# A two-block transformer on one core: the modulation's matrix-vector product moves from VectorE and GpSimd to ScalarE and GpSimd, and to other stages

## Chip, cores and metric

One Trainium2 chip, one of its cores. The metric is the device time of one execution in microseconds (us). Five engines run side by side: TensorE (PE, with its weight loads as PEld), VectorE (DVE), ScalarE (ACT), GpSimd (POOL) and SyncE (SP), whose queue issues the DMAs of this kernel. Each engine works through its own instructions in a fixed order; semaphores hold it until what it needs is there. An "issue" of a DMA stands in SP's order just like an instruction.

## What is computed

1024 tokens of width 1024 in fp32 pass through a first block (differential attention over 4 heads, neighbourhood attention over 8 heads, an output projection, a gate) and then through two layers of a second block. Each of those layers is modulated by a vector that depends on the condition `c` alone:

```python
c_act = jax.nn.silu(c)                                   # (1, 1024)
for l in range(DEPTH_2):                                 # 2 layers
    mod = c_act @ w_mod[l] + b_mod[l]                    # (1, 6144); w_mod[l] is 1024 x 6144
    sh1, sc1, gt1, sh2, sc2, gt2 = jnp.split(mod, 6, axis=-1)
    h = rms_norm_2(x, g_norm_mix[l]) * (1.0 + sc1[:, None]) + sh1[:, None]
    ...                                                  # dilated attention, latent attention (MLA)
    x = x + gt1[:, None] * mix
    h = rms_norm_2(x, g_norm_mlp[l]) * (1.0 + sc2[:, None]) + sh2[:, None]
    y = jnp.square(jax.nn.relu(h @ w_mlp_in[l])) @ w_mlp_out[l]
    x = x + gt2[:, None] * y
```

The change concerns `c_act @ w_mod[l]`, 2 x 24 MB of weights that are read once.

## The kernel before

The stages follow each other: set-up; differential attention (`diff_groups`); neighbourhood attention (`na_groups`); output projection and gate of the first block (`block1_end`); then for each layer dilated attention, latent attention (`mla`), an output projection and the MLP with an up and a down part. All large products run as three passes of split fp32 ("hi" and "lo" tiles): ACT casts a tile to its hi part (`split`, L127, tiles named `ph` in the attention stages), DVE subtracts to get the lo part (L128, `pl`), and PE uses both. In the attention stages a group goes through scores on PE, a minimum on DVE (`add_min`, L493, `mn`), an exponential on ACT, transposes on PE, `split`, and the product with the values on PE.

A modulation *piece* (`mod_piece`) is 256 rows by 256 columns of `w_mod`, 256 KB: one DMA into a tile `modraw` (two chunks of 128 rows), a multiplication of each chunk by its column of `csil` (silu of `c`), and sums into an accumulator `macc` of 128 x 256. Four pieces (kh = 0 to 3) make a column of 256 outputs, 24 columns a layer, 2 layers: 192 pieces. After the fourth piece two transposes of `macc` on PE (L155) and a reduction on DVE (L161) add up the 128 rows, and L974 adds the result to `mod`.

Pieces wait in a list (`background`), and `run_background(n)` writes down the next n of them at a given point of the program. Before the change: 2 after each of the 16 groups of the differential attention and 1 after each of the 16 groups of the neighbourhood attention; 3 in each of the 16 steps (`side`) of output projection and gate; 8 for each of the up part's loops in layer 0's MLP. So the first 48 pieces run in block 1's attention, 48 in its projection and gate, and layer 1's 96 in layer 0's MLP. In the differential attention they are multiplied (L960) and added (L962, L963) on POOL, everywhere else on DVE, which multiplies and adds in one instruction (L967 for the first chunk, L969).

`side` also makes the position tables of the dilated attention: 32 tiles `tab` on DVE (L1156), which have two buffers and leave by the DMA `acd<-tab`. The output projection adds its result to the stream on DVE (L872, tile `xT`).

The order on each engine is not written by hand: a scheduler places every instruction by the program's order as priority and by when it finds its inputs and buffers free. It may so place a piece earlier than the point where the program writes it.

## Time and profile before

| | us |
|---|---|
| median of 3 runs | 3877.02 (3874.85 to 3882.91) |
| the profiled execution | 3880.11 |
| its span | 3878.2 |
| PE busy in it | 3613.2 (93%) |
| DVE | 2821.6 (73%) |
| ACT | 1842.2 (48%) |
| POOL | 1565.9 (40%) |
| layer 0's MLP, layer 1's MLP (from the last instruction of the projection, L874, to the last of L1831) | 1714.8 to 2437.9, 3176.4 to 3871.3 |

Matmuls are pipelined, so a busy PE says little by itself; a stage's length, and what PE waits for in it, say more. "A <- B" in a row means that A waited for B. The two layers of the second block are the same program on other weights, which makes them comparable stage by stage.

### The profile page before, as it was taken

To read this page: it belongs to the slowest core of one execution; us is meant where nothing else is said; L and a number is where in the kernel's file an instruction comes from. 1 tells how busy PE (TensorE), PEld (TensorE's weight loads), DVE (VectorE), ACT (ScalarE), POOL (GpSimd) and SP (SyncE) were. 2 spreads that over 40 slices of the span, in tenths; PEclk is the share of its full clock that TensorE was granted. 3 is DMA by queue.
4 is the path that set the end of the run, shared out by engine and by line. 5 is a ranking of instruction groups with operands and counts; after the bars stand their busy time and mean duration, and the time that the engine had idled before them with its cause. 6 is when DMAs were issued, how large, how long until landed. Compare 5 with 4: busy or idle time off the path is not lost.

```text
span 3878.2 us, 59074 instructions
## 1 busy us (share of the span) xinstructions
PE 3613.2 (93%) x20508; PEld 3097.2 (80%) x20508; DVE 2821.6 (73%) x6304; ACT 1842.2 (48%) x3671; POOL 1565.9 (40%) x1317
## 2 busy tenths in 40 slices
PE   7999899989899899988998999899899998998999
PEld 6988899768899888777786777899788776886777
DVE  5888877667666788658889986666788646447885
ACT  4555555623455678533333333455677633333331
POOL 2334222322322223235337895422133235339882
PEclk9999999999899999999999999999999999999999
DMA  6322323575445500224555323455500132334322
GB/s 193 100 76 74 81 75 83 152 254 183 120 143 152 161 11 25 65 94 144 187 185 193 114 90 108 124 142 156 159 14 26 53 106 101 109 122 147 104 93 82
DMA packets 374077, 446.17 MB, mean 115 GB/s; under 512 B 50037, under 2 KB 246532, under 8 KB 373780
## 3 DMA queue, kind: packets, MB, share of 16 engines
q1 hardware_dynamic: 373780, 442.41, 36.7%
q8 instruction: 162, 2.65, 0.3%
q14 instruction: 135, 1.11, 0.1%
HBM read 312.17 MB, written 101.54 MB: 107 GB/s over the span
## 4 chain that ended last, share of the span: by engine, by line
PE 59%; DVE 16%; POOL 8%; DMA 8%; issue 5%; ACT 4%; SPq 1%; DVEq 0%; ACTq 0%; POOLq 0%
PE pg L183 8%; PE pg L184 8%; PE pg L185 8%; PE sps L1709 8%; PE pg L1709 6%; PE sps L459 2%; PE pt L155 2%; PE pt L693 2%; PE sps L460 2%; DVE macc L969 2%; PE sps L183 2%; DMA modraw<-in_w_mod_dram 2%; PE sps L184 2%; PE pa L700 2%; PE sps L185 2%
## 5 line engine op out<-in xcount | busy, mean ns | idle before, releaser
L209 POOL TENSOR_TENSOR wl<-raw,wh 128x512 fp32r<-128x512 f32 (+2 forms) x234 | 302.5, 1304 | 578.0 <-ACT wh L208 492.7
L128 DVE TENSOR_TENSOR pl<-pt,ph 128x512 fp32r<-128x512 f32 (+3 forms) x406 | 267.6, 665 | 85.8 <-ACT ph L127 77.3
L127 ACT CAST ph<-pt 128x512 fp32r<-128x512 f32 (+3 forms) x406 | 226.0, 574 | 136.1 <-PE pt L693 52.3
L208 ACT CAST wh<-raw 128x512 fp32r<-128x512 f32 (+2 forms) x234 | 138.1, 611 | 221.4 <-DMA raw<-in_w_out_dram 69.5
L969 DVE SCALAR_TENSOR_TENSOR macc<-modraw,csil,macc 128x256 f32<-128x256 f32 x280 | 205.3, 733 | 47.9 <-DMA modraw<-in_w_mod_dram 43.2
L459 PE MATMUL sps<-ks,qs 128*128 128x512 f32 (+3 forms) x480 | 195.8, 410 | 18.5 <-DVE mn L493 10.3
L1698 DVE TENSOR_TENSOR wl<-ssum,wh 128x1024 fp32r<-128x1024 f32 x116 | 168.6, 1453 | 47.5 <-ACT wh L1697 47.5
L1697 ACT CAST wh<-sraw 128x1024 fp32r<-128x1024 f32 x116 | 97.0, 836 | 221.8 <-PE sps L1709 121.4
L1684 POOL TENSOR_TENSOR ssum<-sraw 128x512 f32<-128x512 f32 x58 | 79.0, 1362 | 288.6 <-DVE wl L1698 122.7
L407 POOL TENSOR_TENSOR qn<-qn,r 128x512 f32<-128x512 f32 x64 | 68.8, 1080 | 266.5 <-DVE r L122 109.6
L460 PE MATMUL sps<-kl,qs 128*128 128x512 f32 (+3 forms) x480 | 175.4, 367 | 0.0
L1697 ACT CAST wh<-ssum 128x1024 fp32r<-128x1024 f32 x116 | 121.4, 1047 | 108.9 <-PE pg L1709 79.4
L1643 ACT ACTIVATE xm<-xm,mn 128x1024 f32<-128x1024 f32 x128 | 148.4, 1159 | 32.6 <-DVE mn L493 32.5
L493 DVE CUSTOM_DVE_ANT_0 xd<-sps,dtab 128x256 f32<-128x256 f32 (+1 forms) x256 | 103.3, 412 | 80.1 <-PE sps L460 72.0
L459 PEld LDWEIGHTS sps<-ks,qs 128*128 128x128 f32 x480 | 108.2, 225 | 28.5 <-DVE mn L493 15.0
L1698 POOL TENSOR_TENSOR wl<-sraw,wh 128x512 fp32r<-128x512 f32 x58 | 87.4, 1507 | 90.0 <-ACT wh L1697 81.4
L1698 DVE TENSOR_TENSOR wl<-sraw,wh 128x1024 fp32r<-128x1024 f32 x58 | 94.4, 1628 | 32.0 <-ACT wh L1697 23.9
L700 PE MATMUL pa<-pl,vpm 128*128 128x512 f32 x256 | 109.2, 427 | 2.9 <-DVE pl L128 2.7
L460 PEld LDWEIGHTS sps<-kl,qs 128*128 128x128 f32 x480 | 110.8, 231 | 1.3
L699 PE MATMUL pa<-ph,vpm 128*128 128x512 f32 x256 | 109.2, 427 | 0.6 <-ACT ph L127 0.2
L493 DVE CUSTOM_DVE_ANT_0 xm<-sps,zeros,mn 128x512 f32<-128x512 f32 x128 | 95.3, 745 | 13.8 <-PE sps L185 12.3
L693 PE MATMUL pt<-ident,xm 128*128 128x128 f32 x688 | 104.6, 272 | 0.6 <-DVE pl L128 0.6
(1483 smaller groups left out, 13960.6 us busy)
## 6 DMA issues: line engine op xcount, KB each, us to landing
modraw<-in_w_mod_dram SPq DMA_DIRECT2D x192, 256.0 KB
ud<-r SPq DMA_DIRECT2D x128, 256.0 KB
sraw<-in_w_mlp_in_dram SPq DMA_DIRECT2D x60, 512.0 KB
sraw<-in_w_mlp_out_dram SPq DMA_DIRECT2D x56, 512.0 KB
raw<-in_w_in_dram SPq DMA_DIRECT2D x194, 128.0 KB
uq<-ud SPq DMA_DIRECT2D x96, 256.0 KB
ks<-khh SPq DMA_DIRECT2D x128, 128.0 KB
dtab<-awd SPq DMA_DIRECT2D x32, 512.0 KB
```

Source lines behind the costliest of these rows:

```text
L127: nc.scalar.copy(hi, src)
L128: nc.vector.tensor_tensor(lo, src, hi.bitcast(F32), op=OP.subtract)
L183: nc.tensor.matmul(ps, lh, rh, start=start, stop=False)
L184: nc.tensor.matmul(ps, lh, rl, start=False, stop=False)
L185: nc.tensor.matmul(ps, ll, rh, start=False, stop=stop)
L209: nc.gpsimd.tensor_tensor(wl[:, sl], raw, wh[:, sl].bitcast(F32), op=OP.subtract)
L459: nc.tensor.matmul(ps, self.Q[m][:, q], self.K[m][:, k], start=True, stop=False)
L460: nc.tensor.matmul(ps, self.Q[m][:, q], self.KL[m][:, k], start=False, stop=True)
L969: nc.vector.scalar_tensor_tensor(acc, raw[:, k], c, acc, op0=OP.mult, op1=OP.add)
L1697: nc.scalar.copy(wh[:, 0:m], x)
L1698: (nc.vector if i < 3 else nc.gpsimd).tensor_tensor(wl[:, 0:m], x, wh[:, 0:m].bitcast(F32), op=OP.subtract)
L1709: nc.tensor.matmul(ps, x[:, k, cols], y, start=start and k + n == 0, stop=(k, n) == (nk - 1, 2), skip_group_check=True)
```

## The change

All pieces are multiplied on ACT (two instructions of 128 x 256, in place, scale from `csil`) and added on POOL (two additions, one for kh = 0). The sums over rows become entries of their own in the list, two pieces later. `modraw` has two buffers and `macc` three in every stage. The list is filled for layer 0 at the start and for layer 1 after block 1. Entries are run 4 per group in both attentions of block 1, 3 per group in the dilated attention (32 groups a layer) and 2 per group in the latent attention (16 groups a layer); none in output projection, gate or MLP. In the changed file the lines of a helper stand one to three lower (L127 becomes L126); the new multiplication is L958, the additions L963 and L964.

```diff
-                    yield pre if n == 0 else [], *g[n], after[n] + [lambda u=u: self.run_background(2 if u < 4 else 1)]
+                    yield pre if n == 0 else [], *g[n], after[n] + [lambda u=u: self.run_background(4)]
...
         def side():
             for _ in range(min(per, len(tables))):
                 tables.pop(0)()
-            self.run_background(3)
...
+    def mod_queue(self, l):
+        self.macc = {}
+        for col in range(25):
+            for kh in range(4):
+                if col < 24:
+                    self.background.append(lambda l=l, col=col, kh=kh: self.mod_piece(l, col, kh))
+                if kh == 2 and col:
+                    self.background.append(lambda l=l, col=col: self.mod_sum(l, col - 1))
...
     def mod_piece(self, l, col, kh):
         raw = self.mraw[0].tile([P, 2, 256], F32, tag=self.mraw[1], name="modraw")
         self.dma(raw, self.A["w_mod_2"][l, kh * 256:kh * 256 + 256, col * 256:(col + 1) * 256].rearrange("(k p) e -> p k e", p=P))
+        for k in range(2):
+            nc.scalar.activation(raw[:, k], raw[:, k], AF.Copy, scale=self.csil[:, 2 * kh + k:2 * kh + k + 1])
         if kh == 0:
-            self.macc = self.mp.tile([P, 256], F32, tag="macc", name="macc")
-        acc = self.macc
-        if self.mod_pool:
-            nc.gpsimd.tensor_tensor(raw, raw, self.csil[:, 2 * kh:2 * kh + 2].unsqueeze(2).to_broadcast([P, 2, 256]), op=OP.mult)
-            if kh:
-                nc.gpsimd.tensor_tensor(acc, acc, raw[:, 0], op=OP.add)
-            nc.gpsimd.tensor_tensor(acc, acc if kh else raw[:, 0], raw[:, 1], op=OP.add)
-        for k in () if self.mod_pool else range(2):
-            c = self.csil[:, 2 * kh + k:2 * kh + k + 1]
-            if kh == 0 and k == 0:
-                nc.vector.tensor_scalar(acc, raw[:, k], c, None, op0=OP.mult)
-            else:
-                nc.vector.scalar_tensor_tensor(acc, raw[:, k], c, acc, op0=OP.mult, op1=OP.add)
-        if kh < 3:
-            return
+            self.macc[l, col] = self.mp.tile([P, 256], F32, tag="macc", name="macc")
+        acc = self.macc[l, col]
+        if kh:
+            nc.gpsimd.tensor_tensor(acc, acc, raw[:, 0], op=OP.add)
+        nc.gpsimd.tensor_tensor(acc, acc if kh else raw[:, 0], raw[:, 1], op=OP.add)
+
+    def mod_sum(self, l, col):
+        nc = self.nc
+        acc = self.macc.pop((l, col))
         m = self.mod[l][:, 2 * col:2 * col + 2]
         t = self.sum_rows(acc, 2)
         nc.vector.tensor_tensor(m, t, m, op=OP.add)
...
-                    yield before if n == 0 else [], *g, after[n]
+                    yield before if n == 0 else [], *g, after[n] + [lambda: self.run_background(3)]
...
-                        yield [pre] if half == 0 else [], *self.mla_group(l, hp, m, half, T, cur), after[2 * m + half]
+                        yield [pre] if half == 0 else [], *self.mla_group(l, hp, m, half, T, cur), after[2 * m + half] + [lambda: self.run_background(2)]
...
                 up_rest(fg, w, up_first(fg, w, up), up)
-                self.run_background(8)
...
-            self.mp = self.pool("mp", es, {"mraw": 1})
+            self.mp = self.pool("mp", es, {"mraw": 2, "macc": 3})
...
+                if l == 0:
+                    self.mp = self.pool("mp2", es, {"mraw": 2, "macc": 3})
+                    self.mraw = (self.mp, "mraw")
+                    self.mod_queue(1)
                 self.dilated(a, l)
```

What the scheduler makes of it, at three places. First ACT's order in layer 0's dilated attention (`xd` are exponentials, `ph` the casts that PE waits for, `oT`, `oTc` copies of PE's results). Before:

```order
L1347 ACTIVATE xd,stw<-xd,stw 128x256 x3
L1347 ACTIVATE xd,stw<-xd,stw 128x192
L208 CAST wh<-raw 128x512
L1392 COPY oT<-pa 128x512
L127 CAST ph<-pt 128x512 x2
L1347 ACTIVATE xd,stc<-xd,stc 128x256 x4
L395 ACTIVATE sq<-pg 128x512
```

Now:

```order
L1344 ACTIVATE xd,stw<-xd,stw 128x256 x3
L1366 COPY oTc<-pa 128x2x256
L958 ACTIVATE modraw<-modraw,csil 128x256 x4
L394 ACTIVATE sq<-pg 128x512
L126 CAST ph<-pt 128x512 x2
L958 ACTIVATE modraw<-modraw,csil 128x256 x2
L1344 ACTIVATE xd,stw<-xd,stw 128x256 x3
```

One or two pieces now stand ahead of a pair of casts. Over the whole of ACT's order, 58 pieces come before the last exponential of the differential attention, 52 more before the output projection, 71 in the dilated and 11 in the latent attention.

Second, SP's order between the neighbourhood attention and the first loads `xo` of the output projection (`pled` stores and `w_out` loads belong to gate and projection; `wmask`, `cmult`, `pz` are the first loads of the position tables). Before:

```order
L108 DMA raw<-in_w_out_dram 128x2x256
L108 DMA pled<-pt 128x512 x3
L108 DMA wmask<-c_wmask 128x256
L108 DMA pled<-pt 128x512
L108 DMA cmult<-c_cmult 128x512
L108 DMA pz<-in_positions_dram 128x1
```

Now:

```order
L107 DMA modraw<-in_w_mod_dram 128x2x256 x6
L107 DMA pled<-pt 128x512 x4
L107 DMA raw<-in_w_out_dram 128x2x256
L107 DMA pled<-pt 128x512
L107 DMA raw<-in_w_out_dram 128x2x256
L107 DMA pled<-pt 128x512 x3
L107 DMA raw<-in_w_out_dram 128x2x256 x2
L107 DMA xo<-xTd_97 128x512 x2
L107 DMA wmask<-c_wmask 128x256
L107 DMA cmult<-c_cmult 128x512
L107 DMA pz<-in_positions_dram 128x1
```

Fourteen pieces of layer 1 have been placed at the end of the neighbourhood attention, ahead of the point where the program writes them, and the tables' first loads now stand behind `xo`.

Third, DVE's order in the output projection. Before:

```order
L1145 TENSOR_TENSOR aw<-aw,wmask 128x256
L969 SCALAR_TENSOR_TENSOR macc<-modraw,csil,macc 128x256
L1156 SCALAR_TENSOR_TENSOR tab<-cmult,ac 128x512
L969 SCALAR_TENSOR_TENSOR macc<-modraw,csil,macc 128x256
L1156 SCALAR_TENSOR_TENSOR tab<-cmult,ac 128x512
L969 SCALAR_TENSOR_TENSOR macc<-modraw,csil,macc 128x256 x2
L1143 MEMSET aw 128x256
L969 SCALAR_TENSOR_TENSOR macc<-modraw,csil,macc 128x256
L872 TENSOR_TENSOR xT_10430<-pg,xo 128x512
```

Now:

```order
L1142 TENSOR_TENSOR aw<-aw,wmask 128x256
L1153 SCALAR_TENSOR_TENSOR tab<-cmult,ac 128x512 x3
L870 TENSOR_TENSOR xT_10854<-pg,xo 128x512
L1153 SCALAR_TENSOR_TENSOR tab<-cmult,ac 128x512 x4
L870 TENSOR_TENSOR xT_10855<-pg,xo 128x512
L1153 SCALAR_TENSOR_TENSOR tab<-cmult,ac 128x512 x3
```

The pieces are gone from between the tables; the tables still stand, three and four together, ahead of the additions `xT`.

## Rows read from the trace of the kernel before

**Rows 1.** The page's chain that ended last: shares of the span by engine.

```profile
PE 59%; DVE 16%; POOL 8%; DMA 8%; issue 5%; ACT 4%; SPq 1%; DVEq 0%; ACTq 0%; POOLq 0%
```

**Rows 2.** Windows by stage: length, busy PE, PEld, DVE, ACT, POOL; PE clock, DMA share, GB/s.

```profile
110.00:480.00 370.00, 345.11 (x2554) 321.45 (x2552) 316.75 (x1097) 199.99 (x424) 140.03 (x139) 0.97 0.30 81
480.00:782.00 302.00, 285.65 (x2030) 262.06 (x2030) 217.56 (x677) 173.83 (x396) 86.74 (x85) 0.99 0.38 106
782.00:885.00 103.00, 89.15 (x373) 71.92 (x374) 73.14 (x126) 27.70 (x49) 25.36 (x19) 0.92 0.75 242
885.00:978.00 93.00, 91.03 (x408) 74.98 (x407) 66.71 (x123) 29.90 (x49) 28.00 (x21) 0.97 0.58 187
978.00:1350.00 372.00, 345.62 (x2477) 324.55 (x2476) 255.05 (x823) 202.03 (x513) 88.15 (x101) 0.97 0.49 145
1350.00:1632.00 282.00, 274.17 (x1644) 230.29 (x1644) 231.64 (x560) 212.45 (x418) 81.36 (x103) 0.99 0.08 28
1731.00:2078.00 347.00, 320.40 (x1356) 258.11 (x1355) 296.30 (x379) 121.28 (x180) 159.69 (x109) 0.95 0.54 176
3193.00:3516.00 323.00, 304.67 (x1313) 248.12 (x1311) 176.63 (x170) 118.74 (x176) 151.41 (x106) 0.98 0.36 122
```

**Rows 3.** L1736 in both up parts: ns min/median/max, first and last start in us.

```profile
L1736 DVE TENSOR_TENSOR r<-pg,keep x30: 676/683/692, 1742.7 to 2078.0; 128x512 f32<-128x512 f32 x30
...
L1736 DVE TENSOR_TENSOR r<-pg,keep x30: 678/692/692, 3204.3 to 3516.0; 128x512 f32<-128x512 f32 x30
```

**Rows 4.** L1831, the down part's last tile, in both layers.

```profile
L1831 DVE SCALAR_TENSOR_TENSOR b23l<-pg,mod,b23l x8: 735/738/743, 2123.3 to 2437.9; 128x512 f32<-128x512 f32 x8
...
L1831 DVE SCALAR_TENSOR_TENSOR b23l<-pg,mod,b23l x8: 735/738/750, 3555.1 to 3871.3; 128x512 f32<-128x512 f32 x8
```

**Rows 5.** Groups on DVE, layer 0's up part: busy us, mean ns | idle before, releasers.

```profile
L969 DVE SCALAR_TENSOR_TENSOR macc<-modraw,csil,macc 128x256 f32<-128x256 f32 x145 | 117.6, 811 | 28.6 <-DMA modraw<-in_w_mod_dram 25.7 <-DVE r L1736 0.3
```

**Rows 6.** Additions of block 1's and layer 0's projection, the tables, PE's wait in 782:885.

```profile
L872 DVE TENSOR_TENSOR xT<-pg,xo x16: 676/682/693, 786.8 to 882.9; 128x512 f32<-128x512 f32 x16
...
L874 DVE SCALAR_TENSOR_TENSOR xT<-pg,mod,xo x16: 737/750/751, 1631.9 to 1714.8; 128x512 f32<-128x512 f32 x16
...
L1156 DVE SCALAR_TENSOR_TENSOR tab<-cmult,ac x32: 675/692/1787, 772.5 to 859.6; 128x512 f32<-128x512 f32 x32
...
PE pg L183 <- DVE xT L872: 16.2, 5, 7.8
```

**Rows 7.** The moved sum on PE, by time in layer 0's up part: start, us.

```profile
1808.50 0.38 PE L155 MATMUL pt<-ident,macc 128*128 128x128 f32 x2
...
1808.95 0.40 PE L1709 MATMUL pg<-a70h,wh 128*128 128x512 f32 x1
1809.18 0.40 PE L1709 MATMUL pg<-a70l,wh 128*128 128x512 f32 x1
```

**Rows 8.** ACT groups of 128 x 256 by form: busy us, mean ns | idle.

```profile
L1347 ACT ACTIVATE xd<-xd,stc 128x256 f32<-128x256 f32 x128 | 63.6, 505 | 17.9 <-DVE stc L1345 17.8
```

**Rows 9.** The old pieces on POOL: ns min/median/max.

```profile
L960 POOL TENSOR_TENSOR modraw<-modraw,csil x32: 1039/1042/1421, 70.0 to 420.4; 128x512 f32<-128x512 f32 x32
...
L962 POOL TENSOR_TENSOR macc<-macc,modraw x24: 727/740/1739, 83.5 to 421.5; 128x256 f32<-128x256 f32 x24
```

**Rows 10.** A piece late on DVE, by time; its waits in 480:782 (us, times).

```profile
464.50 0.48 DVE L969 SCALAR_TENSOR_TENSOR macc<-modraw,csil,macc 128x256 f32<-128x256 f32 x1 [2.11 <-DMA modraw<-in_w_mod_dram]
...
465.64 0.39 PE L184 MATMUL pa<-pl,vp 128*128 128x256 f32 x1 [1.82 <-DVE pl L128]
...
  DMA modraw<-in_w_mod_dram: 10.2, 6
```

**Rows 11.** DVE beside POOL: two by time; L120 in 978:1350, ns min/median/max.

```profile
470.01 2.07 POOL L624 TENSOR_TENSOR edge<-edge,colmask 128x896 f32<-128x896 f32 x1
470.11 1.99 DVE L591 TENSOR_TENSOR ga<-ip,gb 128x4 f32<-128x4 f32 x1
...
L120 DVE TENSOR_TENSOR rst<-rsy x66: 153/166/1216, 994.8 to 1342.5; 128x8 f32<-128x8 f32 x48, 128x4 f32<-128x4 f32 x15, 128x24 f32<-128x24 f32 x3
```

More of the change, by code (lines that the diff above doesn't have):

```diff
@@ L946, in mod_start @@
                 self.columns(self.gmix[:, l, i, :], A[n][l].rearrange("(k p) -> k p", p=P), 8)
-        for l in range(2):
-            for col in range(24):
-                for kh in range(4):
+        self.mod_queue(0)
+    def mod_queue(self, l):
[3 more added lines that the diff above has]
+                if col < 24:
                     self.background.append(lambda l=l, col=col, kh=kh: self.mod_piece(l, col, kh))
+                if kh == 2 and col:
+                    self.background.append(lambda l=l, col=col: self.mod_sum(l, col - 1))
     def mod_piece(self, l, col, kh):
@@ L1785, in mlp @@
             self.sring[t].insert(0, sr1)
-        self.mraw = (self.wp, "raw")
         for f in steps[4:]:
@@ L1849, in mlp @@
             up = self.pool("uu", eu, {"r": 4})
-            self.mp = self.mq
             up_rest(1, w, x, up)
@@ L1929, in emit @@
                 es.close()
+                if l == 0:
+                    self.mp = self.pool("mp2", es, {"mraw": 2, "macc": 3})
+                    self.mraw = (self.mp, "mraw")
+                    self.mod_queue(1)
                 self.dilated(a, l)
                 self.mla(l)
+                es.close()
                 self.open_mlp(es)
```

6 lines of the change are left out of this document (removed).

## Prediction

> **What bounds the kernel now.** First the chain of work that ended last: PE has 59% of it, DVE 16%, POOL and DMA 8% each [rows 1]. So the kernel is bound by TensorE, with DVE next. Such shares are means over unlike stages; the second view is therefore the windows [rows 2], where the reader is to compare PE's busy time with the length of each stage. In the attention stages PE is busy 345 of 370, 286 of 302, 346 of 372 and 274 of 282 us: they are PE's, with 16 to 26 us idle each, 8 in the latent attention. In the first block's projection (782 to 885) it is busy 89 of 103, and DVE works next to the busiest DMA share of the run (0.75). The last two windows are the up part of layer 0's MLP, which carries layer 1's pieces, and the same part of layer 1, which carries none: 347 against 323 us, DVE busy 296 against 177. Third, the rows of single lines say what that difference is made of.
>
> **The change part by part, against the profiled 3880.1 us** (3.1 above the median of 3877.0).
>
> *MLP of layer 0, all 96 pieces gone.* From the first to the last L1736 it takes 335.3 us with pieces and 311.7 without [rows 3], 23.6 less. In between, 145 of DVE's L969 were busy 117.6 us and waited 28.6 more, nearly all of it for `modraw` [rows 5]: with its other work that fills DVE's window. From there to the last tile of the down part it is 359.9 and 355.3 us [rows 3, 4], another 4.6; but behind the first half layer 0 also starts the next layer's norm, which layer 1 has not, so I take half. **-26**, between -24 and -28.
>
> *Projection and gate, 48 pieces gone.* The 16 additions of the projection take 96.1 us from first to last, the same 16 of layer 0's projection 82.9 [rows 6]: 13.2 to be had, and PE waited 16.2 us in five waits for `xT`. But pieces are not alone on that DVE. The 32 tables run from 772.5 to 859.6, 2.7 us each, while one takes 0.69: they wait for their two buffers to be written out. In the new order their first loads stand behind `xo`, so they start later (I allow 10 us), and the last four stand ahead of the twelfth addition. Their pace should rise, since some 24 pieces of 256 KB leave a stretch with DMA at 0.75 [rows 2]. I take **-8**, between -13 and +8 (tables at the old pace, 10 us later, now late by that much). The gate has PE busy 91 of 93 us [rows 2]: **-1**, between -2 and 0.
>
> *Sums over rows.* 12 of the 48 stay in block 1's attention; 36 move there or into layer 0's attention, in stages where PE is the bound. Two transposes and the matmul behind them take 0.45 us, the matmul alone 0.23 [rows 7], so a sum costs PE 0.22 us: **+8**, between 0 (in PE's idle time) and 8. Before, they were inside the two terms above.
>
> *Neighbourhood attention without DVE's pieces.* There 16 pieces cost DVE two instructions each, and it stood 10.2 us waiting for `modraw` in six waits [rows 10]; what of it reached PE I put at **-4**, between -8 and 0.
>
> *The pieces' new work.* On ACT two instructions of 128 x 256 each. Before, no such product is on ACT; the nearest row, an exponential of the same size, takes 0.505 us [rows 8], so a piece is 1.0 us. On POOL an addition is 0.74 [rows 9], 1.75 of them a piece: 1.3 us. By the counts of the new order, ACT rises from 200 to 258 of 370 us in the differential, from 174 to 226 of 302 in the neighbourhood, from 202 to 273 of 372 in the dilated and from 212 to 223 of 282 in the latent attention [rows 2]. POOL stays in the differential attention at its 140 (an old piece there was 1.04 + 1.3) and goes to about 155, 180 and 95. All this lies beside PE's work. That such loads can be borne is read from the latent attention: ACT at 75% and DVE at 82% leave PE 97% busy. So busy time as such I cost at nothing; what covers it is PE's own queue, and without that cover the ACT part alone would be 192 us.
>
> What isn't free is order. Each engine takes its instructions in line, so a piece whose `modraw` is late holds the casts `ph` behind it, then DVE's `pl`, then PE. The trace has one such event: DVE waits 2.11 us for `modraw`, `pl` is behind it, and PE stands 1.82 us [rows 10]. With two buffers, in the MLP, the wait was 25.7 us over 145 L969, of which a column's four pieces have seven, so 83 pieces [rows 5]: 0.31 us a piece. For 192 pieces that is 60 us on ACT. Of it between nothing and 1.82/2.11 reach PE, 0 to 52 us; in the neighbourhood attention DVE stood 10.2 us and PE was idle 16 for all reasons together [rows 2, 10], so most of such waits are covered. I take a quarter, **+15**.
>
> POOL's own consumers (`qn`, `mix`, weights' lo parts) and the SP queue now stand behind additions too: a late addition frees `modraw` late, and on SP six loads in a row stand ahead of `pled` and `w_out` at the end of the neighbourhood attention. There, and where POOL holds DVE: two instructions that start within 0.1 us of each other end together, DVE's with 128 x 4 elements after 1.99 us beside POOL's 2.07, and a small L120 takes 0.17 us in the median but 1.22 at most [rows 11]. POOL gains some 124 additions in the dilated attention; if each holds one DVE instruction for half its 0.74 us, DVE gains 46 us there and stands at 84%, still under PE. **+4**, between 0 and 15.
>
> The Trainium skill has this as a rule ("SBUF — State Buffer", section "SBUF: two separate sides"): DVE with two SBUF inputs and a GpSimd instruction that reads SBUF share a port pair, and whichever starts first keeps it to its end. [Rows 11] agree. By that rule alone every addition would be a full block of 0.74 us; the third rival below is made of it.
>
> A second rule of the Trainium skill speaks against the change ("ScalarE: Activation LUTs", section "Rules for kernel authors"): multiplications and additions belong on VectorE. By busy time that holds here too: two L969 of 0.48 us [rows 10] against 2.3 us on two engines, and if engine time were the bound the change would cost 192 x 1.3 = 250 us. [Rows 2] say it isn't, so the sum doesn't use it.
>
> **Sum:** -26 - 8 - 1 + 8 - 4 + 15 + 4 = -12, so 3868 as this execution, **3865 as a median**.
>
> **Rivals.** *Covered:* ACT and POOL cost PE nothing and the projection gets its 13: -26 - 13 - 1 + 8 - 4 = -36, 3841. For it: the latent attention's loads. Against: the event of [rows 10], and the tables.
>
> *ACT becomes the one that holds the line, slower:* the pieces wait on ACT as they did on DVE and each wait reaches PE at 1.82/2.11, in the differential attention above all, where one piece falls on every 6 us and two buffers must be loaded, multiplied and added in turn. -26 + 0 - 1 + 8 - 4 + 52 + 4 = +33, 3910. It decides from the point where the pieces cost PE over 0.16 us each: the gains less the sums' shift, 26 + 8 + 1 + 4 - 8 = 31 us, by 192. Against: casts of one group are rarely the next thing PE needs.
>
> *POOL holds DVE, and the tables keep their pace:* a quarter of DVE's 46 us reaches PE (+12), and the projection gains nothing: -26 - 1 + 8 - 4 + 15 + 12 = +4, 3881. In this case the change moves the loss instead of removing it.
>
> *It doesn't do what it says:* the scheduler might put pieces back into projection or MLP. The order shows none there; only the fourteen early ones. I give this nothing.
>
> **How the numbers follow.** About 0.2%, 7.8 us, is what a measurement of this kernel can tell from no change. The forecast has 0.46 (of that 0.34 faster by more than 7.8, 0.12 within), "covered" 0.15, "ACT holds the line" 0.21 (0.18 slower, 0.03 within), "POOL and tables" 0.18 (0.10 within, 0.08 slower). Faster 0.49, same 0.25, slower 0.26. The range goes from a little below "covered" (3836) to 3900, short of the worst of the ACT case; the forecast's own is 3848 to 3880.
>
> **What the profile will show.** Right: layer 0's up part, first to last L1736, at about 312 us like layer 1's; the projection's additions in about 88 us; dilated attention of layer 0 longer by 5 to 15 us, ACT busy some 270 us there, with waits for `modraw` of some 60 us in all on ACT. Wrong: if ACT's waits for `modraw` pass 100 us and PE's waits for `ph` and `pl` grow with them; if the tables end the projection's window as before; or if the up part keeps its 335 us, which would mean that something else than the pieces held it.

## The result and the profile after

The changed kernel takes 3912.2 us in the median of four runs (3905.4 to 3918.1), the kernel before 3876.1 beside it: ratio 1.0089, 95% interval 1.0069 to 1.0109. It is **slower by 36 us**; the forecast was 12 us faster, and the upper end of its range, 3900 us, is passed too. The profiled execution (3912.2) has a span of 3910.5 us.

Windows by stage, with the events that bound them: from the first L542 (now L541) of the differential attention to the first exponential of the neighbourhood attention; to its last exponential; to the last addition of the gate; then the dilated attention of layer 0, first to last exponential; to the last exponential of the latent attention; and layer 0's up part, first to last L1736 (now L1733). Columns as in [rows 2]. The kernel before:

```profile
114.80:473.90 359.10, 336.78 (x2508) 314.70 (x2507) 307.24 (x1057) 194.82 (x411) 136.40 (x136) 0.98 0.30 80
473.90:747.70 273.80, 258.87 (x1884) 239.48 (x1885) 202.91 (x650) 159.26 (x371) 78.73 (x78) 0.98 0.36 98
747.70:976.70 229.00, 209.32 (x931) 170.50 (x930) 158.18 (x299) 72.85 (x128) 60.82 (x45) 0.95 0.65 209
1053.00:1332.40 279.40, 272.53 (x1947) 256.06 (x1946) 191.77 (x664) 164.66 (x438) 54.51 (x69) 0.99 0.56 165
1332.40:1617.90 285.50, 271.71 (x1648) 229.47 (x1646) 237.38 (x587) 216.33 (x437) 88.06 (x110) 0.98 0.08 28
1742.70:2078.00 335.30, 314.40 (x1338) 254.56 (x1338) 284.60 (x372) 113.17 (x167) 149.11 (x102) 0.96 0.56 182
```

The changed kernel:

```profile
118.30:483.90 365.60, 338.70 (x2494) 316.68 (x2493) 305.27 (x1053) 234.57 (x510) 130.93 (x139) 0.97 0.34 94
483.90:776.00 292.10, 270.85 (x1900) 246.18 (x1899) 208.68 (x645) 193.32 (x464) 137.31 (x165) 0.95 0.43 119
776.00:1004.40 228.40, 211.54 (x912) 171.25 (x912) 109.10 (x178) 76.70 (x140) 63.57 (x50) 0.95 0.48 154
1080.40:1376.90 296.50, 280.17 (x1942) 256.99 (x1940) 207.39 (x691) 208.47 (x553) 134.34 (x179) 0.98 0.70 211
1376.90:1677.60 300.70, 282.74 (x1698) 236.40 (x1698) 252.21 (x611) 234.40 (x486) 114.21 (x147) 0.97 0.14 44
1803.70:2115.80 312.10, 302.17 (x1296) 247.84 (x1296) 166.85 (x165) 110.99 (x164) 141.55 (x99) 0.97 0.37 126
```

The last line is the gain: 335.3 to 312.1 us. The window from the neighbourhood attention's end through projection and gate gained nothing (229.0 to 228.4). The four attention windows lost 6.5, 18.3, 17.1 and 15.2 us, 57 in all. Their nature is read from two columns. Length less PE busy is PE's idle time: 57.9 us before, 82.4 now, so 24.5 more. The rest, 32.6 us, is PE being busy longer, with the same products but for the sums. Length times one less the granted clock, by these two digits, is 21 us before and 40 now: some 19 us of it go with the lower clock.

Where [rows 3] and [rows 6] stood, and the new ACT work (group line, with mean ns, idle time before it and releasers):

```profile
L1733 DVE TENSOR_TENSOR r<-pg,keep x60: 676/691/693, 1803.7 to 3549.5; 128x512 f32<-128x512 f32 x60
L870 DVE TENSOR_TENSOR xT<-pg,xo x16: 676/680/690, 811.4 to 911.6; 128x512 f32<-128x512 f32 x16
L1153 DVE SCALAR_TENSOR_TENSOR tab<-cmult,ac x32: 675/692/1790, 821.1 to 890.7; 128x512 f32<-128x512 f32 x32
PE pg L182 <- DVE xT L870: 13.6, 8, 3.8
L958 ACT ACTIVATE modraw<-modraw,csil 128x256 f32<-128x256 f32 x384 | 175.3, 506 | 113.1 <-DMA modraw<-in_w_mod_dram 106.2 <-POOL inner L625 5.0 <-POOL macc L963 0.6
```

A multiplication costs 0.506 us, as priced by an exponential [rows 8]; the waits for `modraw` are 106 us, not 60.

One such wait, in the dilated attention: ACT, then one row of DVE, then PE (start, length, and in brackets the idle time before), then windows over it.

```profile
1324.67 0.91 ACT L958 ACTIVATE modraw<-modraw,csil 128x256 f32<-128x256 f32 x2 [1.54 <-DMA modraw<-in_w_mod_dram]
1325.49 0.49 ACT L207 CAST wh<-raw 128x384 fp32r<-128x384 f32 x1
1325.89 0.57 ACT L126 CAST ph<-pt 128x512 fp32r<-128x512 f32 x1
...
1325.52 0.75 DVE L130 SCALAR_TENSOR_TENSOR cl<-pg,lg,ch 128x512 fp32r<-128x512 f32 x1 [2.87 <-DMA qs<-qhh]
...
1326.52 0.38 PE L1362 MATMUL pa<-ph,v 128*128 128x256 f32 x1 [1.17 <-ACT ph L126]
1328.28 0.39 PE L458 MATMUL sps<-ks,qs 128*128 128x256 f32 x1 [1.38 <-DVE mn L492]
...
1320.00:1326.00 6.00, 5.34 (x39) 4.71 (x37) 3.05 (x8) 2.49 (x6) 0.68 (x1) 1.00 0.87 238
1326.00:1330.00 4.00, 2.10 (x9) 1.62 (x10) 3.97 (x16) 2.45 (x5) 2.46 (x4) 0.94 0.74 235
1330.00:1333.00 3.00, 3.00 (x9) 2.34 (x8) 2.90 (x15) 2.20 (x7) 0.73 (x1) 0.51 0.88 220
1333.00:1340.00 7.00, 7.00 (x43) 6.13 (x42) 5.22 (x17) 4.47 (x12) 3.24 (x4) 1.00 1.02 335
```

ACT stands 1.54 us for a load; the multiplications, a weight cast and only then `ph` follow; PE waits 1.17 us for `ph`. Soon it waits 1.38 us more, for the minimum `mn` on DVE; that second wait goes back to another DMA: DVE had stood 2.87 us for `qs<-qhh`. After both waits PE's clock stands at the lower level (0.51, 1.2 GHz) for 3 us, in which it works on 9 products; in the next 7 us, at 2.4 GHz, on 43 (some of these are half as wide). So here time was lost in the waits and again behind them. The chain that ended last has the loads in that stage too (start, length, what):

```profile
1176.41 4.79 DMA modraw<-in_w_mod_dram
1181.29 0.91 ACT modraw L958 x2
1182.74 0.74 POOL macc L964
1183.50 3.10 DMA modraw<-in_w_mod_dram
```

Load, multiply, add, and the freed buffer's next load follow one another: the pieces themselves have become a chain. What such a chain costs it doesn't say; that takes the runs below.

### The profile page after: what moved, and what is told of

It is laid out like the page before. It is cut to its first block, busy times and chain, and to the rows that moved or that the text cites. A ratio compares the mean times of both kernels' runs of the same rounds, so it can differ in the third digit from the quotient of the medians.

```text
span 3910.5 us, 59657 instructions
## 1 busy us (share of the span) xinstructions
PE 3641.4 (93%) x20508; PEld 3113.1 (80%) x20508; DVE 2662.4 (68%) x5984; ACT 1986.7 (51%) x4055; POOL 1727.5 (44%) x1565
## 4 chain that ended last, share of the span: by engine, by line
PE 58%; DVE 13%; POOL 9%; DMA 8%; ACT 5%; issue 5%; SPq 1%; POOLq 0%; ACTq 0%; DVEq 0%
PE sps L1706 9%; PE pg L182 7%; PE pg L183 7%; PE pg L184 7%; PE pg L1706 7%; PE pt L692 2%; PE pt L154 2%; PE sps L458 2%; DMA modraw<-in_w_mod_dram 2%; PE sps L182 2%; PE sps L183 2%; PE pa L699 2%; PE sps L459 2%; PE sps L184 2%; PE pa L698 2%
## 5 line engine op out<-in xcount | busy, mean ns | idle before, releaser
L127 DVE TENSOR_TENSOR pl<-pt,ph 128x512 fp32r<-128x512 f32 (+3 forms) x411 | 270.2, 663 | 95.0 <-ACT ph L126 87.9
L126 ACT CAST ph<-pt 128x512 fp32r<-128x512 f32 (+3 forms) x411 | 227.9, 570 | 119.3 <-PE pt L692 47.2
L207 ACT CAST wh<-raw 128x512 fp32r<-128x512 f32 (+2 forms) x234 | 137.5, 607 | 196.7 <-DMA raw<-in_w_out_dram 57.9
L958 ACT ACTIVATE modraw<-modraw,csil 128x256 f32<-128x256 f32 x384 | 175.3, 506 | 113.1 <-DMA modraw<-in_w_mod_dram 106.2
L458 PE MATMUL sps<-ks,qs 128*128 128x512 f32 (+3 forms) x480 | 197.3, 413 | 24.5 <-DVE mn L492 18.0
L963 POOL TENSOR_TENSOR macc<-macc,modraw 128x256 f32<-128x256 f32 x144 | 110.4, 767 | 156.3 <-ACT modraw L958 141.0
L1733 DVE TENSOR_TENSOR r<-pg,keep 128x512 f32<-128x512 f32 x60 | 41.4, 690 | 124.5 <-PE pg L1706 124.5
L964 POOL TENSOR_TENSOR macc<-macc,modraw 128x256 f32<-128x256 f32 x144 | 106.9, 743 | 12.3 <-ACT modraw L958 1.8
```

The source lines that it names most:

```text
L126: nc.scalar.copy(hi, src)
L127: nc.vector.tensor_tensor(lo, src, hi.bitcast(F32), op=OP.subtract)
L458: nc.tensor.matmul(ps, self.Q[m][:, q], self.K[m][:, k], start=True, stop=False)
```

## The experiments

Eighteen runs in five batches, each batch on one chip; a ratio is against the kernel before on that chip, with its 95% interval.

### Taking parts away

`e1_no_pieces`:

```diff
     def mod_piece(self, l, col, kh):
         nc = self.nc
+        return
...
     def mod_sum(self, l, col):
         nc = self.nc
-        acc = self.macc.pop((l, col))
-        m = self.mod[l][:, 2 * col:2 * col + 2]
-        t = self.sum_rows(acc, 2)
-        nc.vector.tensor_tensor(m, t, m, op=OP.add)
```

> Leaves out the whole modulation product (no loads, no multiplications, no additions, no sums over rows; the modulation is its bias alone). It is the floor under all 192 pieces. In the changed kernel the MLP gained 28.6 us against the kernel before, and set-up, attention stages and projection lost some 64 us. If the pieces themselves cost that, the floor is 3876 - 29 = 3847 us or a little lower, since the pieces of the kernel before in attention and projection go too: 3830 to 3850 us. If part of the loss comes from the new order alone (the position tables that now start behind xo), the floor lies above 3850 us.

3830.3 us, ratio 0.9864 (0.9848 to 0.9879). Its five windows:

```profile
114.20:455.70 341.50, 329.17 (x2497) 309.51 (x2495) 290.29 (x1032) 194.51 (x407) 59.90 (x49) 1.00 0.23 60
455.70:727.60 271.90, 258.51 (x1875) 237.58 (x1876) 194.85 (x619) 160.64 (x374) 81.69 (x87) 0.98 0.32 86
727.60:947.50 219.90, 205.14 (x914) 167.38 (x912) 110.12 (x177) 73.64 (x130) 59.95 (x45) 0.98 0.48 155
1023.40:1309.80 286.40, 277.61 (x1914) 259.77 (x1913) 190.06 (x657) 161.58 (x431) 54.74 (x69) 0.96 0.55 161
1309.80:1594.90 285.10, 274.61 (x1681) 232.47 (x1679) 239.52 (x595) 219.33 (x444) 87.57 (x110) 0.99 0.09 28
```

So all pieces cost the kernel before 1.36%, 53 us, and the changed kernel 2.25%, 87: it is the pieces that cost, and not the new order without them. The dilated attention takes 286.4 us without any piece and 279.4 in the kernel before, which has none there either: something other than the pieces, most likely the scheduler's order, moves that stage by 7 us, and no stage is read closer than that below. Of the 7 us, 5 are PE busy longer, at a granted clock of 0.96 against 0.99, with 8.8 us idle against 6.9: the clock moves without the pieces too.

`e1_loads`: the same, but with the return behind `self.dma(raw, ...)`.

> Leaves out multiplications, additions and sums; only the 192 loads of 256 KB remain, at the places of the changed kernel. Theory 'ACT holds the line' (late modraw in ACT's order holds casts) and theory 'POOL holds DVE' (the additions): no more than 10 us above the floor of the run without pieces. Theory 'loads' (DMA traffic, and six loads in a row on SP ahead of what the stages need): 30 us or more above the floor.

3904.6 us, 1.0047 (1.0030 to 1.0064), which looked like "loads". It isn't what was meant: with no reader, a buffer is free as soon as it is written, and the scheduler put all 192 loads into set-up and differential attention. The row of the loads, and SP's longest wait there:

```profile
L107 SPq DMA_DIRECT2D modraw<-in_w_mod_dram x192: 367/368/1470, 32.6 to 413.9; - x192
...
SPq L107 <- DMA modraw<-in_w_mod_dram: 167.9, 146, 4.3
```

The differential attention took 396 us (first to last `x` on L541), 74 more than without pieces; behind it no stage was over 3.1 us longer than without pieces. Inconclusive, but it shows what loads that wait in SP's order can cost.

`e1_no_mult`:

```diff
-        for k in range(2):
-            nc.scalar.activation(raw[:, k], raw[:, k], AF.Copy, scale=self.csil[:, 2 * kh + k:2 * kh + k + 1])
```

> Leaves out the multiplications by silu(c) on ACT; loads, additions on POOL and sums over rows remain. Theory 'ACT holds the line': 35 us or more below the changed kernel's 3912 us, so 3877 us or less, since ACT waits for no modraw any more. Theory 'POOL holds DVE': within 15 us of 3912 us, with POOL now the one that waits for modraw.

3885.4 us, 1.0008 (0.9998 to 1.0019): 0.81%, 31 us, below the changed kernel. Places stayed. The loads are as late as before, only POOL waits for them now:

```profile
  DMA modraw<-in_w_mod_dram: 129.9, 76
```

That fits "ACT holds the line", a little under its 35 us: late loads seem to cost less where POOL waits than where ACT does. But the run also takes the 175 us of multiplications off ACT, so it doesn't tell the waits from the work.

`e1_no_adds`: the same as `e1_loads`, with the return behind the multiplications.

> Leaves out the additions on POOL and the sums over rows; loads and the multiplications on ACT remain. Theory 'ACT holds the line': still 3890 us or more, with 80 us or more of waits for modraw on ACT. Theory 'POOL holds DVE': 30 us or more below 3912 us, so 3882 us or less. Since modraw comes free earlier without additions, waits on ACT may fall a little under either.

3873.4 us, 0.9973 (0.9961 to 0.9985). Inconclusive too: of its 192 loads the scheduler put 147 before the differential attention's last `x`, and none into layer 0's attention.

### Buffers, queues, engines

`e2_pool_queue`:

```diff
-        self.dma(raw, self.A["w_mod_2"][l, kh * 256:kh * 256 + 256, col * 256:(col + 1) * 256].rearrange("(k p) e -> p k e", p=P))
+        nc.gpsimd.dma_start(raw, self.A["w_mod_2"][l, kh * 256:kh * 256 + 256, col * 256:(col + 1) * 256].rearrange("(k p) e -> p k e", p=P))
```

> The changed kernel with the 192 loads of modraw issued on POOL's queue instead of SP's, behind the additions that free their buffer. Theory 'SP's line' (in the attention stages SP stands some 330 us at modraw loads until an addition on POOL frees the buffer, and loads of queries, keys and weights stand behind): 30 us or more below 3912 us, so 3882 us or less. Theory 'POOL's line' (additions, and what they wait for, hold POOL's own work and DVE): no gain, 3905 us or more, since POOL gets the issues too. Theory 'ACT holds the line': no gain or a loss, as modraw comes later.

3932.4 us, 1.0131 (1.0110 to 1.0153): slower. "SP's line" falls. Its trace gives what the others leave out, the loads' time from issue to landing:

```profile
DMA to landing us min/median/max: 3.0/3.6/8.3
```

`e2_bufs4`, in both pools:

```diff
-{"mraw": 2, "macc": 3}
+{"mraw": 4, "macc": 3}
```

> The changed kernel with four buffers of modraw instead of two. Theory 'SP's line': 20 us or more below 3912 us, SP's waits for additions at least halved. Theory 'ACT holds the line': 15 us or more below, with ACT's 106 us of waits for modraw under 40 us. Theory 'POOL's line': within 10 us of 3912 us.

3911.9 us, 1.0074 (1.0052 to 1.0096): no difference from the changed kernel. Nor did the waits go; see below.

`e2_macc6`:

```diff
-{"mraw": 2, "macc": 3}
+{"mraw": 2, "macc": 6}
```

> The changed kernel with six accumulators instead of three (the scheduler then puts some pieces earlier). POOL waits 44 us in the differential attention for transposes on PE that free an accumulator. Theory 'POOL's line': 10 us or more below 3912 us, in the differential attention above all. Theories 'SP's line' and 'ACT holds the line': within 10 us of 3912 us.

3918.3 us, 1.0094 (1.0076 to 1.0112): nothing gained; accumulators aren't it.

`e2_dve`, at the new places:

```diff
-            nc.scalar.activation(raw[:, k], raw[:, k], AF.Copy, scale=self.csil[:, 2 * kh + k:2 * kh + k + 1])
...
-        if kh:
-            nc.gpsimd.tensor_tensor(acc, acc, raw[:, 0], op=OP.add)
-        nc.gpsimd.tensor_tensor(acc, acc if kh else raw[:, 0], raw[:, 1], op=OP.add)
+        for k in range(2):
+            c = self.csil[:, 2 * kh + k:2 * kh + k + 1]
+            if kh == 0 and k == 0:
+                nc.vector.tensor_scalar(acc, raw[:, k], c, None, op0=OP.mult)
+            else:
+                nc.vector.scalar_tensor_tensor(acc, raw[:, k], c, acc, op0=OP.mult, op1=OP.add)
```

> The changed kernel with each piece multiplied and added on DVE in two instructions, as the kernel before does in most stages, at the places of the changed kernel; nothing of a piece on ACT or POOL. Theory 'POOL's line': 30 us or more below 3912 us. Theory 'any work of this size in the attention stages costs it' (places, not engines): 3900 us or more, as DVE gets 0.9 us a piece. Theory 'SP's line': between, 3885 to 3900 us, since buffers come free after 0.9 us instead of some 2.3 us.

3907.8 us, 1.0063 (1.0043 to 1.0083). The same cost on another engine, within the intervals (10 us apart, good to some 11): so the cost doesn't need ACT or POOL. By itself that doesn't say that each engine costs it by the same path. DVE now waits in line, 56.2 us for `modraw` in 45 waits.

### Halves, and loads written ahead

`e3_ahead`:

```diff
+        first = 4 * col + kh
+        for i in range(0 if first == 0 else first + 3, min(first + 4, 96)):
+            self.mod_load(l, i // 4, i % 4)
+        raw = self.raws.pop((l, col, kh))
...
-            self.mp = self.pool("mp", es, {"mraw": 2, "macc": 3})
+            self.mp = self.pool("mp", es, {"mraw": 4, "macc": 3})
```

> The changed kernel with four buffers of modraw and each load written three pieces ahead of its use (four buffers alone left the load some 3.6 us ahead of its use, as before, and the time where it was). Theory 'late loads' (ACT and POOL wait in line for modraw, and casts and weights behind them reach PE): ACT's waits for modraw fall from 106 us to under 30 us, and the time by 25 us or more, to 3887 us or less. Theory 'places' (any work of this size in attention stages that PE fills disturbs its order, whatever engine and buffers): within 10 us of 3912 us although the waits go.

3907.5 us, 1.0063 (1.0045 to 1.0081). The waits didn't go, so the theories weren't told apart. From the 192 issues on SP and the first multiplication of each piece: the median distance was some 3.0 to 4.4 us by attention stage in the changed kernel, 3.6 to 5.3 with four buffers, 3.6 to 5.4 with loads written ahead. So an earlier load only brought an earlier multiplication: the scheduler lets it follow as soon as it expects the load to have landed.

`e3_second_only` is the kernel before with `old_piece` (its `mod_piece`) for layer 0 and the changed one's list and pieces for layer 1; `e3_first_only` is the changed kernel with the opposite:

```diff
-                    self.mod_queue(1)
+                    for col in range(24):
+                        for kh in range(4):
+                            self.background.append(lambda col=col, kh=kh: self.old_piece(1, col, kh))
...
                 up_rest(fg, w, up_first(fg, w, up), up)
+                self.run_background(8)
```

> Block 1 as in the kernel before; only layer 1's 96 pieces move from layer 0's MLP to layer 0's attention, on ACT and POOL. By stages of the changed kernel this part gives 28.6 us in the MLP and costs 17 + 8 + 7 = 32 us in the dilated attention, the transition and the latent attention: +4 us, within 10 us of the kernel before. If the loss there came only from the pieces put early or from the late tables of the changed kernel: 15 us or more faster than before.

> Block 1 as in the changed kernel (96 pieces in its attention on ACT and POOL, none in projection and gate); layer 1's 96 pieces on DVE in layer 0's MLP as in the kernel before. By stages: 12 us in set-up and differential attention, 16 in the neighbourhood attention, about nothing net from there to the dilated attention, and the MLP unchanged: 25 us or more slower than before. With the 14 early pieces gone, the neighbourhood attention may give back some 5 of these.

3895.1 us, 1.0029 (1.0019 to 1.0040), and 3896.8 us, 1.0030 (1.0019 to 1.0041): 11 and 12 us slower. Neither half pays. The first is some 7 us above what its stages gave; the second is well under its 25, although its neighbourhood attention takes 288.0 us, 14 more than before: from there to the dilated attention's first exponential it gave 9 us back. The halves add to 23 of the 35 us; the other 12, good to some 10 by the intervals, come with having both, and stay open.

`e3_before_ahead`, against the kernel before:

```diff
-        self.mp = self.pool("mp2", es, {"mraw": 3})
+        self.mp = self.pool("mp2", es, {"mraw": 4})
...
-        self.mraw = (self.wp, "raw")
...
-            self.mp = self.mq
+            self.mp = self.pool("mp3", eu, {"mraw": 4})
+            self.mraw = (self.mp, "mraw")
...
+        first = 4 * col + kh
+        for i in range(first if first % 48 == 0 else first + 3, min(first + 4, first - first % 48 + 48)):
+            self.mod_load(l, i // 4, i % 4)
```

> The kernel before, engines and places unchanged, with four buffers of modraw in every stage and each load written three pieces ahead of its use. Theory 'late loads': DVE's 28.6 us of waits in layer 0's MLP and most of the 42 us on POOL go, and the kernel is 15 us or more faster than before. Theory 'places': the MLP keeps its 335 us and the time stays within 8 us.

3867.2 us, **0.9957** (0.9941 to 0.9973): 17 us faster than before. Layer 0's up part:

```profile
1742.10:2068.70 326.60, 312.12 (x1343) 253.80 (x1342) 284.63 (x383) 113.63 (x166) 151.63 (x103) 0.96 0.59 190
```

326.6 against 335.3 us; another 4.8 came from the down part. DVE's waits for `modraw` in the up part, 26.0 us before, are gone, and load and use lie 10.1 us apart in the median there instead of 5.0. Buffers and earlier loads came together, so they aren't told apart. And with no such wait left, the up part is still 14.5 us longer than without pieces (312.1): that much their loads and work cost even there.

### Load and use set apart

`e4_late_use`: `e3_ahead` and a hold in ACT's order (`issue_after` keeps the scheduler from placing an instruction ahead of another one of the same engine):

```diff
-            nc.scalar.copy(hi, src)
+            self.last_cast = nc.scalar.copy(hi, src).ins
...
+        with self.tc.issue_after(self.last_cast) if self.last_cast is not None else ExitStack():
+            for k in range(2):
+                nc.scalar.activation(raw[:, k], raw[:, k], AF.Copy, scale=self.csil[:, 2 * kh + k:2 * kh + k + 1])
```

> The changed kernel with four buffers of modraw, each load written three pieces ahead, and each pair of multiplications held in ACT's order behind the last cast written before it, so that a multiplication can't follow its load at once. (Written ahead alone, the multiplication moved ahead with its load: ACT still waited 70 us for modraw.) Theory 'late loads': ACT's waits for modraw fall under 25 us and the time by 25 us or more against the changed kernel, to 3887 us or less. Theory 'places' (the work itself in stages that PE fills): the waits fall and the time stays at 3900 us or more.

3885.0 us, 0.9999 (0.9988 to 1.0010): 0.90%, 35 us, below the changed kernel by the ratios, with every instruction of it still there. The two were not run on one chip; their medians are 27 us apart and their profiled executions 25. ACT's groups with four buffers, with loads ahead, and with load and use apart:

```profile
L958 ACT ACTIVATE modraw<-modraw,csil 128x256 f32<-128x256 f32 x384 | 172.6, 507 | 83.0 <-DMA modraw<-in_w_mod_dram 80.3 <-POOL wl L208 1.7 <-POOL macc L963 0.5
```

```profile
L966 ACT ACTIVATE modraw<-modraw,csil 128x256 f32<-128x256 f32 x384 | 174.1, 510 | 72.9 <-DMA modraw<-in_w_mod_dram 70.2 <-POOL macc L972 1.2 <-POOL macc L971 0.5
```

```profile
L968 ACT ACTIVATE modraw<-modraw,csil 128x256 f32<-128x256 f32 x384 | 163.3, 504 | 11.6 <-DMA modraw<-in_w_mod_dram 11.4
```

Issue and use now lie 12 to 40 us apart in the median, by attention stage. Its attention windows:

```profile
116.50:476.00 359.50, 340.23 (x2516) 317.68 (x2514) 307.72 (x1054) 232.97 (x507) 128.68 (x135) 0.97 0.34 93
476.00:762.80 286.80, 263.93 (x1895) 242.97 (x1895) 196.82 (x645) 191.16 (x455) 134.93 (x161) 0.96 0.44 121
1061.40:1359.20 297.80, 281.26 (x1954) 261.82 (x1952) 209.84 (x692) 215.42 (x574) 145.81 (x195) 0.97 0.73 220
1359.20:1655.30 296.10, 278.33 (x1685) 233.57 (x1684) 247.08 (x609) 234.39 (x486) 114.34 (x148) 0.98 0.13 42
```

Of the traces' 25 us, 22 came from block 1 (6, 5, and 6 more up to the gate) and the latent attention (5). Two reservations: the hold also took most of the 14 early pieces back into the dilated attention, and that stage kept its 298 us. So there it isn't the waits that cost, although the loads had 14.3% of that stage's chain in the changed kernel and have 2.5% here; the total is what is shown.

`e4_loads_held` is `e1_loads` with

```diff
-        self.nc.sync.dma_start(out, in_)
+        self.last_dma = self.nc.sync.dma_start(out, in_).ins
...
+        with self.tc.issue_after(self.last_dma):
+            self.dma(raw, self.A["w_mod_2"][l, kh * 256:kh * 256 + 256, col * 256:(col + 1) * 256].rearrange("(k p) e -> p k e", p=P))
```

and `e4_no_adds_held` is that with the multiplications held as above.

> Leaves out multiplications, additions and sums over rows, like the run with loads alone, but each load is held in SP's order behind the last DMA written before it, so that the loads stay in the groups of the changed kernel and don't crowd into the differential attention. Theory 'loads' (traffic, and SP's line): 25 us or more above the 3830 us of the run without pieces. Theories of ACT, POOL and PE: no more than 10 us above it, 3840 us or less.

> Leaves out the additions on POOL and the sums over rows; loads and multiplications on ACT stay in the groups of the changed kernel (loads held behind the last DMA, multiplications behind the last cast written before). With the run before this one it gives what ACT's part costs. Theory 'ACT holds the line': 30 us or more above the loads alone. Theory 'POOL and PE' (additions and sums are what costs): within 15 us of the loads alone.

3851.5 us, 0.9915 (0.9895 to 0.9934), and 3858.3 us, 0.9940 (0.9917 to 0.9962). Loads alone cost 0.51%, 20 us, between what the two theories wanted; the multiplications 0.25%, 10 us, far from 30 and not clear of nothing. With the run before them this makes a ladder, each step good to some 9 to 12 us by the intervals:

| | ratio | step, us |
|---|---|---|
| no pieces | 0.9864 | |
| loads, held | 0.9915 | 20 |
| and multiplications, held | 0.9940 | 10 |
| and additions and sums (use held; load ahead) | 0.9999 | 23 |
| the changed kernel: use right behind load | 1.0089 | 35 |

The steps aren't pure. With loads and multiplications held, ACT still waits for `modraw`:

```profile
  DMA modraw<-in_w_mod_dram: 64.7, 45
```

So its 10 us hold these waits too, and the next step goes to a run with 11.4 us of them and four buffers: it isn't additions and sums alone. The last step is 25 us by the traces. What ACT's waits cost by themselves therefore stays open; that the pieces cost some 53 us even with load and use apart doesn't.

### Fewer pieces per stage

`e4_spread`, against `e3_before_ahead`:

```diff
-                    yield pre if n == 0 else [], *g[n], after[n] + [lambda u=u: self.run_background(2 if u < 4 else 1)]
+                    yield pre if n == 0 else [], *g[n], after[n] + [lambda u=u: self.run_background(1 if u < 4 else 1)]
...
-                self.run_background(8)
+                self.run_background(2 if l else 8)
```

> A candidate: the kernel before with four buffers and loads written ahead (3867 us), and fewer pieces in the differential attention: one instead of two a group there, as the last vector of layer 0 (its gate of the MLP, 16 pieces) is only needed at the end of layer 0's MLP and moves into that MLP's up part, and that of layer 1 likewise into layer 1's. By the run without pieces the 32 pieces of the differential attention cost 22 us; if cost goes with the number, half of it, 8 to 12 us, goes: 3855 to 3860 us. If 96 pieces of another kind in the up part cost more than before, nothing is gained.

3882.6 us, 0.9991 (0.9981 to 1.0001): a miss. The first window is what was hoped for, 348.2 us against 362.0 in `e3_before_ahead`:

```profile
116.90:465.10 348.20, 332.56 (x2495) 310.84 (x2494) 302.00 (x1047) 193.81 (x406) 85.82 (x79) 0.99 0.27 71
```

But eight entries in each of layer 0's 14 loops are 112, just what was left in the list, so layer 1's last vector didn't get to layer 1: all 112 pieces ran in layer 0's MLP, 37 of DVE's instructions for them in the down part, which grew from 355.0 to 369.6 us.

`e5_ahead_held` holds DVE's multiply-adds as ACT's were (first part); `e5_dil_held` adds one piece a group in the differential attention, and the second part:

```diff
+            with self.tc.issue_after(self.last_dve) if self.last_dve is not None else ExitStack():
...
+                    yield before if n == 0 else [], *g, after[n] + [lambda n=n: self.run_background((n + 1) % 2 if l == 0 else 0)]
...
+                self.run_background(2 if l else min(7, len(self.background) - 16))
```

> The kernel before with four buffers, loads written three pieces ahead (3867 us), and each multiply-add on DVE held in its order behind the last subtraction or squared activation written before it, so that load and use stand apart. Places and numbers of pieces as before. Theory 'late loads', which the changed kernel bore out when load and use were set apart (27 us): DVE's waits for modraw in layer 0's up part go, its 326.6 us fall to 320 or less, and the time is 5 us or more below 3867 us. If the pieces' time on DVE is what holds the up part: no change against 3867 us.

> The same with fewer pieces at a time: one instead of two a group in the differential attention, the last vector of layer 0 (16 pieces) at every other group of layer 0's dilated attention, and the last vector of layer 1 (16 pieces) in layer 1's up part, so that 80 instead of 96 run in layer 0's MLP. With one a group the differential attention cost 13 us less in the run before this one, where however all 112 remaining pieces went into layer 0's MLP, spilled into its down part and cost 15 us there. If cost goes with the number in a stage: 10 us or more below the run with 96 in layer 0's MLP, about 3850 us. If 16 pieces in the dilated attention cost what 71 did per piece or more: no more than 5 us below it.

3885.9 us, 1.0004 (0.9995 to 1.0012): a miss, 18 us slower than `e3_before_ahead` where 5 us faster was expected; and 3863.8 us, **0.9945** (0.9933 to 0.9956), the fastest version, 22 us below `e5_ahead_held`, but only 3 to 5 us below `e3_before_ahead`, with overlapping intervals, where 10 was hoped for. The pieces in the dilated attention aren't why: with 15 of them there, held, and no wait for `modraw`, it takes 277.6 us, against 278.1 without any in `e3_before_ahead`. The up part got shorter, 323.1 us (not the 320 expected) and, with 80 pieces, 317.2. The hold did harm elsewhere: from the neighbourhood attention's end to the dilated attention's first exponential `e5_ahead_held` takes 320.4 us, `e3_before_ahead` 301.8. In projection and gate there is seldom a subtraction to be behind, so pieces slid past the gate into the start of the second block. That window (last addition of the gate to the first exponential) in `e5_dil_held`:

```profile
960.40:1060.10 99.70, 71.38 (x494) 67.64 (x495) 67.19 (x167) 31.26 (x52) 27.03 (x21) 0.79 0.31 93
```

73.8 us in `e3_before_ahead`, 99.7 here, with 11 pieces in it. The same places without the hold there weren't tried.

## Why the prediction was wrong

**MLP -26:** right. 23.2 in the up part as forecast, 5.4 behind it, together 28.6; the up part takes 312.1 us as said.

**Projection -8, gate -1:** the projection missed. The tables start at 821.1 instead of 772.5 [rows 6]; half of these 49 us is that the whole projection starts 25 us later, and against its first addition they are 24 us later, where I allowed 10. Their pace rose (70 us for 32 instead of 87), but PE still waits 13.6 us for `xT`, and the additions take 100.2 us instead of 88. Of the ends I had, -13 and +8, it came out at +4 for the additions. The gate gave its 1 us (93.8 to 92.8), and the whole window 1.

**"What of it lies beside PE's work I cost at nothing":** this is the step that failed most. Loads 20 us, multiplications 10, additions and sums 23, each with the reservations above: 53 us by the ladder, for which my sum had 8 (the sums) and 4 (POOL and SP). It is also just what all pieces cost before (1.36%, 53 us): setting them beside PE's work in the attention stages didn't hide them, it moved the bill. In whole: my sum took 39 us off for the pieces' old places and put 27 on for the new ones; without pieces the runs give 53 and 87. By which path loads and work beside it reach PE stays open. The latent attention, from which I read that such loads can be borne [rows 2], showed only that a stage can be dense, not that an addition to it is free.

**ACT's waits, +15:** right in kind, too small. I had 60 us of waits and a quarter reaching PE. They were 106, and setting load and use apart gave 35 us (25 by the traces); leaving the multiplications out gave 31, work and waits together. That is a quarter to a third of the waits, and there were more of them. The path wasn't the one I gave, by `ph` and `pl`. PE's waits in the dilated attention, the first row from the kernel before, the others from the changed one:

```profile
PE sps L459 <- DVE mn L493: 0.4, 1, 0.4
PE sps L458 <- DVE mn L492: 5.4, 5, 2.8
PE pa L1385 <- ACT ph L126: 1.3, 2, 0.9
```

Summed over the four attention windows, PE waits some 57 us before and 82 now, but for `ph` and `pl` together only 14.8 and 17.6; for `mn` 10.9 and 20.3, and for DVE in all 31.7 and 54.9. DVE's own waits for ACT rose from 121 to 151 us, and with load and use apart they are back at 124, while PE's waits for DVE only fall to 49: ACT's late loads do reach DVE, but most of what DVE adds to PE's waits has another cause, which stays open.

**No term for the clock:** the sum counted PE's waits once. In the four attention windows 24.5 us more of idle time came with 19 us by the clock: of 32.6 us more PE busy 8 are for the sums, 19 for the clock, some 6 are left. The Trainium skill has this reckoning ("TensorE: Matmul & The Clock Gate", section "Terms": the penalty is the throttled time by the share of clock withheld). That the waits brought the lower clock is argued, not shown: without pieces PE idles 13 us less in these windows than in the kernel before, and the clock costs some 20 us in both.

**Neighbourhood attention without DVE's pieces, -4:** +18.3 instead; the pieces on ACT and POOL there, 52 by the order, cost far more than 16 on DVE.

**Rivals:** "ACT becomes the one that holds the line" said 3910 us and came nearest, with chance 0.21. Late loads on ACT are borne out for 25 to 35 us of its 52, its path by `ph` and `pl` isn't; the rest of its time was right by accident, as it held nothing for loads and work. "POOL holds DVE" isn't what happened. DVE is busy 15.6 us longer in the dilated attention, for which I had 46 (and 84%, where 255 + 46 of 372 us are 81%), and nearly all of it is the sums' own instructions:

```profile
L160 DVE TENSOR_REDUCE sr<-pj 128x2 f32<-128x256 f32 x17 | 7.1, 416 | 0.4 <-PE pj L154 0.3
L971 DVE TENSOR_TENSOR mod<-sr,mod 128x2 f32<-128x2 f32 x17 | 5.5, 322 | 0.2
```

Pieces on DVE alone, with nothing of them on POOL, cost the same within the intervals (1.0063 against 1.0089). Nor did the rule of the Trainium skill tell here that such work belongs on VectorE ("ScalarE: Activation LUTs", section "Rules for kernel authors"): at these places the engine made no measurable difference. Of what I named as proof against me the first half came, over 100 us of waits on ACT; the second, PE's waits for `ph` and `pl` growing with them, came only by the 3 us above.

## What to carry to other kernels

Work set beside a stage that the matrix engine fills isn't free: price it from a run that leaves it out, not from the idle share of the engine that gets it. The number in a stage counts: in the dilated attention some 60 pieces came with 10 to 17 us, 15 with nothing that could be read. A load that the scheduler lets its use follow at once was often late here, in the order of whatever engine used it. More buffers and earlier loads didn't help where the use moved along (`e3_ahead`) and did where it didn't (`e3_before_ahead`); an edge that keeps the use back helped, if there was something at every place to keep it behind. A chain or a wait that is long isn't yet a cost: look at what PE waits for, and at the run without it. Of waits in a stage that PE fills, look at the clock as well as the wait.

## What was not expected of the hardware

Two waits of PE of 1.17 and 1.38 us within 4 us were followed by 3 us at the lower clock, in a stage where PE is otherwise 95% busy. And a 256 KB load that lands in 3.0 us at best takes 3.6 in the median and 8.3 at most (192 loads on POOL's queue); in the chain of the dilated attention single loads stand with 2.9 to 6.9 us. A use placed three to four us behind its issue was often late: ACT waited 77 times for 192 pieces.
